# Up-projection of a gated MLP: seven block products for all three float32r parts instead of the mixed parts only

## The chip, the cores and the metric

The kernel runs on one core of one Trainium2 chip. The metric is the device time of one execution in microseconds (us); less is better. A run of the kernel before took 2623.07 us in the median.

## The reference

A decoder of two layers, 1,024 tokens, model width 1,024, all in float32: differential attention, then a gated MLP; forgetting attention, then a gated MLP. The change is in the MLP, which runs twice:

```python
def conv_ffn(x, w_in, conv_w, conv_b, w_out):
    u = x @ w_in                       # 1024 x 1024 times 1024 x 5632
    u = causal depthwise convolution of width 3 over the tokens, + conv_b
    gate, val = jnp.split(u, 2, axis=-1)
    return (jax.nn.gelu(gate) * val) @ w_out      # 2816 = 22 * 128
```

x is normalised (RMS norm with a gain) before it, and the output after it.

## The kernel before, in words

**Number format.** TensorE multiplies float32r, a float32 of reduced precision. To keep float32 accuracy every operand is split into two float32r parts, high = round(x) and low = x - high. A product is then three matmuls: high*high, high*low, low*high. One matmul has a 128x128 weight tile, 512 tokens, and sums into one bank of PSUM (128 x 512 float32); there are eight banks.

**Tiles.** `ffn` (L466) goes over 22 pairs j (`NJ`), each of one block of 128 gate columns (v = 0) and one of 128 value columns (v = 1). The 1,024 inputs are eight blocks `kc` of 128 rows; the tokens are two halves of 512. A pair fills four banks, c11, c12 (gate, first and second half), c21, c22 (value); even pairs use banks 0 to 3, odd pairs 4 to 7. So a pair can start while the results of the one before are read.

**Plain pairs** (0 and 1, `products`, L512): 4 quarters x 8 blocks x 3 parts = 96 matmuls.

**Pairs 2 to 21** (`winograd`, L521): the pair is taken as a 2x2 block product, rows gate/value, inner dimension split into blocks 0 to 3 and 4 to 7, columns the token halves. The Strassen-Winograd scheme forms it from seven products of blocks instead of eight. The kernel uses it for the two mixed parts only: `low` (L533) issues one of the seven products for high*low and low*high, 8 matmuls. The high*high part is added in the ordinary way by `main` (L540), four times 8 matmuls. GpSimd forms four weight sums per pair out of the split parts, for the high and the low parts separately (`sums`, L483, 8 instructions of 128x512, one pair ahead); the token sums (`token_sums`, L497) are formed once per layer, 32 instructions. VectorE combines the products in PSUM (`add`, L548).

**After a pair**, `act` (L572) applies the convolution: one ScalarE instruction (L576) and two VectorE `scalar_tensor_tensor` (STT, L578) per half of the pair, gelu on ScalarE (L582), the product gate*value on VectorE (L586), and a store to DRAM.

**Weights.** `Weights` (L30) loads raw float32 tiles of 512 KB from the SyncE queue (`wr`, two buffers) and splits each: high on ScalarE (L73), low on VectorE (L75). The parts have eight buffers `w`: two pairs.

**Tokens.** In front of the MLP `early` (L355) and `second_half` transpose the normalised stream on TensorE (L216), the first half of the tokens during the output projection, the second half after the first halves of the plain pairs. For each block ScalarE writes the high part out of PSUM (L231) and VectorE the low part, with PSUM as one input (L232). These 16 tiles, and e, f, y, the weight sums and more, come out of one pool of 28 buffers, `t`.

**Order.** A planner places the instructions on their engines at build time: it takes the earliest written instruction that is ready by its own costs, and each engine then runs its list strictly in order. Waits are semaphores. The pool buffers limit how far the list of one engine runs ahead.

**Down-projection** (`sweeps`, L374) follows, with all eight banks: for each of four blocks of tokens two banks in turn, the first block with banks 0 and 1.

Of the kernel before, what the change touches and what calls it, by code (L numbers as in the profile page):

```python
# [14 lines left out]
P = 128  # L15
# [8 lines left out]
EPS = 1e-6  # L24
SUB_EPS = 1e-5
LAM0 = 0.8 - 0.6 * math.exp(0.0)
NBUF = {"x": 16, "wr": 2, "w": 8, "t": 28}


class Weights:  # L30
# [6 lines left out]

    def load(self, n):
        while self.loaded < min(n, len(self.reqs)):
            ap, gain, shape = self.reqs[self.loaded]  # L40
            size = shape[0] * shape[1]
            t = self.k.tile("wr", tag="wr")
            self.k.loading = self.k.nc.sync.dma_start(out=t[:, :size], in_=ap)
            self.raw[self.loaded] = t
            self.loaded += 1
            self.gained(self.loaded - 1)

    def gained(self, n):

        while self.gains < n:  # L50
            _, gain, shape = self.reqs[self.gains]
# [38 lines left out]
class Kernel:  # L90
# [119 lines left out]
    def transposes(self, xs, half, kcs, banks, gain):  # L210

        nc = self.nc
        for i, kc in enumerate(kcs):
            b = banks[i % len(banks)]
            for t in range(4):
                nc.tensor.transpose(  # L216
                    self.ps[:, b * HALF + t * P:b * HALF + (t + 1) * P], xs[t][:, kc * P:(kc + 1) * P], self.ident
                )
            if half == 0:
                if kc == 0:  # L220
                    self.xh, self.xl = [], []
                self.xh.append(self.tile("xh", F32R, tag=self.x_tag))
                self.xl.append(self.tile("xl", F32R, tag=self.x_tag))
# [5 lines left out]
            else:  # L229
# [2 lines left out]
                nc.vector.scalar_tensor_tensor(  # L232
                    out=lo, in0=self.bank(b), scalar=g, in1=hi, op0=ALU.mult, op1=ALU.subtract
                )


    def load_post(self, gpost):
# [228 lines left out]
    def ffn(self, l, gpost, h_in, h_out, gain, final):  # L466


        nc = self.nc
        conv = self.const.tile([P, 2 * NJ, 4], F32, tag="conv", name=f"conv{l}")  # L470
        nc.sync.dma_start(out=conv, in_=self.a["conv"][l])
        g_dram = self.dram.tile([2, NJ, P, HALF], F32, name=f"g{l}")
        w_t, s_t = {}, {}
        t_c = {}
        toks = [slice(0, HALF), slice(HALF, S)]
# [7 lines left out]
        def sums(j):  # L483

            t = [self.tile("ws", F32R, [P, 2, 4, P]) for _ in range(4)]
            op = nc.gpsimd.tensor_tensor
            for i in range(2):
                g, v = w_t[j][0][i], w_t[j][1][i]
                a11, a12, a21, a22 = g[:, 0:4], g[:, 4:8], v[:, 0:4], v[:, 4:8]
                s1, s2, s3, s4 = (x[:, i] for x in t)  # L490
                op(out=s1, in0=a21, in1=a22, op=ALU.add)  # L491
                op(out=s2, in0=s1, in1=a11, op=ALU.subtract)  # L492
                op(out=s3, in0=a11, in1=a21, op=ALU.subtract)  # L493
                op(out=s4, in0=a12, in1=s2, op=ALU.subtract)
            s_t[j] = t

        def token_sums(eng, i, kcs):  # L497

            x = (self.xh, self.xl)[i]
            for kc in kcs:  # L500
                b11, b12 = (x[kc][:, c] for c in toks)
                b21, b22 = (x[kc + 4][:, c] for c in toks)
                t12, t34 = (self.tile("xs", F32R, [P, 2, HALF], tag="x") for _ in range(2))
                t_c[i, kc] = [t12[:, 0], t12[:, 1], t34[:, 0], t34[:, 1]]
                t1, t2, t3, t4 = t_c[i, kc]
                op = eng.tensor_tensor
                op(out=t1, in0=b12, in1=b11, op=ALU.subtract)
                op(out=t2, in0=b22, in1=t1, op=ALU.subtract)
                op(out=t3, in0=b22, in1=b12, op=ALU.subtract)
                op(out=t4, in0=b21, in1=t2, op=ALU.subtract)  # L510

        def products(j, v, half):  # L512
            wh, wl = w_t[j][v]
            b = 4 * (j % 2) + 2 * v + half
            for kc in range(8):
                for i, (w, x) in enumerate(((wh, self.xh), (wh, self.xl), (wl, self.xh))):
                    nc.tensor.matmul(  # L517
                        self.bank(b), w[:, kc], x[kc][:, toks[half]], start=kc == 0 and i == 0, stop=kc == 7 and i == 2
                    )

        def winograd(j):  # L521
            base = 4 * (j % 2)
            c11, c12, c21, c22 = (self.bank(base + i) for i in range(4))
            (gh, gl), (vh, vl) = w_t[j]
            s = s_t.pop(j)
            e = self.tile("e", shape=[P, 2, HALF])
            f = self.tile("f", shape=[P, 2, HALF])
            x = lambda half, k0: ([self.xh[k0 + k][:, toks[half]] for k in range(4)],
                                  [self.xl[k0 + k][:, toks[half]] for k in range(4)])
            sw = lambda n: (s[n - 1][:, 0], s[n - 1][:, 1])  # L530
            tw = lambda n: [[t_c[i, k][n - 1] for k in range(4)] for i in range(2)]

            def low(o, w, b, start=False):  # L533
                n = 0
                for k in range(4):
                    for i in range(2):
                        nc.tensor.matmul(o, w[i][:, k], b[1 - i][k], start=start and n == 0, stop=n == 7, skip_group_check=not start)  # L537
                        n += 1

            def main(o, w, half, start=False):  # L540
                for k in range(8):
                    nc.tensor.matmul(  # L542
                        o, w[:, k], self.xh[k][:, toks[half]], start=start and k == 0, stop=k == 7,
                        skip_group_check=not start,
                    )

            g = (gh, gl)
            add = lambda out, a, b: nc.vector.tensor_tensor(out=out, in0=a, in1=b, op=ALU.add)  # L548
            low(c11, [t[:, 0:4] for t in g], x(0, 0), True)
# [12 lines left out]
            main(c12, gh, 1)  # L562
            add(c12, c12, f[:, 0])
            act(j, 0)
            add(c21, c21, f[:, 1])
            main(c22, vh, 1)
            add(c22, c22, e[:, 1])
            act(j, 1)

        g_t = {}  # L570

        def act(j, v):  # L572
# [7 lines left out]
                )  # L580
            if v == 0:
                nc.scalar.activation(out=y, in_=y, func=AF.Gelu_apprx_tanh)  # L582
                g_t[j] = y
            else:
                g = g_t.pop(j)
# [21 lines left out]
            for v in (0, 1):  # L607
                products(j, v, 0)
        self.second_half((1, 3, 5, 7))
        token_sums(nc.gpsimd, 1, (2, 3))  # L610
        for j in range(NJ):
            if j > 0:
                weights(j + 1)
            if j < 2:
                if j == 1:
                    sums(2)
                    token_sums(nc.vector, 1, (0, 1))
                    token_sums(nc.vector, 0, range(4))
                for v in (0, 1):
                    products(j, v, 1)  # L620
                    act(j, v)
            else:
                if j + 1 < NJ:
                    sums(j + 1)
                else:
                    self.sweeps_begin(source, NJ, gpost, h_in, h_out, final)
                winograd(j)
            w_t.pop(j)
        self.sweeps(NJ, gain, final)


# [570 lines left out]
    def requests(self):  # L1202
# [34 lines left out]
        def ffn(l):  # L1237
            for j in range(NJ):
                for g in range(2):
                    r.append((a["ffn_in"][l, 2 * j + g], None, whole))  # L1240
# [152 lines left out]
```

## Time and profile before

| | |
|---|---|
| median of 3 runs | 2623.07 us (2622.27 to 3161.32) |
| the profiled execution | 2620.13 us, span 2618.3 us |
| PE busy | 2537.9 us, 97% of the span |
| DVE (VectorE), ACT (ScalarE), POOL (GpSimd) busy | 1673.3, 1073.0, 895.4 us |
| mean granted TensorE clock | 0.991 of full speed |
| first MLP up-projection, second one | from 568.63 us, from 1911.81 us |

How to read it: PE is TensorE's matmuls, PEld its weight loads. Busy shares are means over the span, so stretches are looked at one by one. Times of rows count from the start of the span. A row of the timeline gives the start, the time taken, engine, line, operation, output<-inputs, the count, and in square brackets the idle time of the engine before it with what released it. A matmul's own time (0.39 us) overlaps with the next one's; the distance between starts is the pace.

### The profile page before, as it was taken

The numbers are of one execution on the slowest core, as the hardware profiler recorded it, in microseconds if no ns is written. First come the engines' busy times: TensorE is split into PE (matmuls) and PEld (weight loads), VectorE is DVE, ScalarE is ACT, GpSimd is POOL, SyncE is SP. The second block draws the span as 40 slices with busy tenths as digits, with TensorE's granted clock in tenths as the row PEclk, the third lists the DMA queues.
The fourth block names the chain that finished last, engine by engine and source line by source line (L and its number), as shares of the span: only waits on it lengthen the run. The fifth ranks groups of instructions, "written<-read, shape, count | busy, mean of one in ns | idle before, by whom it ended". The sixth has DMA issues, their size and how long they took to land. (4 is left out here: it accounts for less than half of the span.)

```text
span 2618.3 us, 34308 instructions
## 1 busy us (share of the span) xinstructions
PE 2537.9 (97%) x13013; PEld 2152.3 (82%) x13013; DVE 1673.3 (64%) x2586; ACT 1073.0 (41%) x1857; POOL 895.4 (34%) x1050
## 2 busy tenths in 40 slices
PE   8999999998999999999999999998998999999998
PEld 7898998786888888888878888876887888888887
DVE  5767677558766767252567877776467676675253
ACT  4555555333323324242445555557332332234232
POOL 1222223227655661010322333223237666550000
PEclk9999999999999999999999999998999999999999
DMA  4111212341222225353312322225412222235353
GB/s 161 43 43 51 55 50 80 109 144 57 84 83 75 81 81 176 131 203 118 116 59 48 57 71 68 50 49 112 154 57 89 73 81 81 81 112 186 110 211 113
DMA packets 119866, 249.00 MB, mean 95 GB/s; under 512 B 34035, under 2 KB 50196, under 8 KB 119700
## 3 DMA queue, kind: packets, MB, share of 16 engines
q1 hardware_dynamic: 119700, 246.81, 29.5%
q8 instruction: 102, 1.67, 0.3%
q14 instruction: 64, 0.52, 0.1%
HBM read 197.85 MB, written 48.92 MB: 94 GB/s over the span
## 5 line engine op out<-in xcount | busy, mean ns | idle before, releaser
L73 ACT CAST wh<-wr 128x1024 fp32r<-128x1024 f32 (+1 forms) x240 | 252.3, 1052 | 800.3 <-PE ps L542 449.2
L75 DVE TENSOR_TENSOR wl<-wr,wh 128x1024 fp32r<-128x1024 f32 (+1 forms) x236 | 301.9, 1281 | 329.4 <-ACT wh L73 271.0
L267 PE MATMUL ps<-wh,src 128*128 128x512 f32 x1408 | 377.1, 389 | 0.0
L542 PE MATMUL ps<-xh,wh 128*128 128x512 f32 x1280 | 310.2, 389 | 1.9 <-DVE y L578 1.9
L267 PEld LDWEIGHTS ps<-wh,src 128*128 128x128 f32 x1408 | 264.2, 188 | 54.7
L542 PEld LDWEIGHTS ps<-xh,wh 128*128 128x128 f32 x1280 | 240.1, 188 | 52.4 <-issue 2.7
L537 PE MATMUL ps<-xs,ws 128*128 128x512 f32 x960 | 235.4, 394 | 16.6 <-POOL ws L492 16.6
L776 POOL CAST qz<-qs 64x128 fp32r<-64x128 f32 x256 | 84.4, 332 | 474.3 <-PE ps L765 439.3
L537 PEld LDWEIGHTS ps<-xs,ws 128*128 128x128 f32 x960 | 182.9, 191 | 55.8 <-POOL ws L492 17.5
L578 DVE SCALAR_TENSOR_TENSOR y<-ps,conv,y 128x1023 f32<-128x1023 f32 (+1 forms) x176 | 220.5, 1273 | 1.3
L267 PE MATMUL ps<-wl,src 128*128 128x512 f32 x704 | 216.7, 389 | 0.0
L204 POOL TENSOR_SCALAR post<-post 128x1 f32<-128x1 f32 x56 | 21.9, 392 | 560.0 <-ACT f L208 559.6
L650 PE MATMUL ps<-xh,wh 128*128 128x512 f32 x512 | 208.2, 407 | 4.8 <-DVE qs L671 4.4
L650 PE MATMUL ps<-xh,wl 128*128 128x512 f32 x512 | 201.4, 393 | 0.0
L650 PE MATMUL ps<-xl,wh 128*128 128x512 f32 x512 | 201.3, 393 | 0.0
L806 DVE TENSOR_TENSOR ptl<-ps,pth 128x512 fp32r<-128x512 f32 (+3 forms) x288 | 152.9, 552 | 60.3 <-ACT pth L805 58.1
L805 ACT CAST pth<-ps 128x512 fp32r<-128x512 f32 (+3 forms) x288 | 131.0, 478 | 63.0 <-PE ps L795 53.4
L267 PEld LDWEIGHTS ps<-wl,src 128*128 128x128 f32 x704 | 132.2, 188 | 27.4
L717 PE MATMUL ps<-wh,xh 128*128 128x256 f32 (+1 forms) x512 | 149.1, 292 | 1.4 <-DVE f L327 0.8
L717 PE MATMUL ps<-wh,xl 128*128 128x256 f32 (+1 forms) x512 | 146.4, 287 | 0.1
L491 POOL TENSOR_TENSOR ws<-wh 128x512 fp32r<-128x512 f32 x40 | 55.5, 1387 | 263.3 <-ACT wh L73 263.3
L717 PE MATMUL ps<-wl,xh 128*128 128x256 f32 (+1 forms) x512 | 145.4, 286 | 0.0
(200 smaller groups left out, 5788.8 us busy)
## 6 DMA issues: line engine op xcount, KB each, us to landing
wr<-in_ffn_in_dram SPq DMA_DIRECT2D x88, 512.0 KB, 3.5
wr<-in_ffn_out_dram SPq DMA_DIRECT2D x88, 512.0 KB, 3.9
g<-y SPq DMA_DIRECT2D x44, 512.0 KB, 2.8
g<-g SPq DMA_DIRECT2D x44, 512.0 KB, 7.0
h<-hold SPq DMA_DIRECT2D x24, 512.0 KB, 2.8
hold<-h SPq DMA_DIRECT2D x24, 512.0 KB, 6.8
crow<-c SPq DMA_DIRECT2D x16, 512.0 KB, 7.4
xraw<-in_x_dram SPq DMA_DIRECT2D x8, 512.0 KB, 6.6
```

Of the source, the lines that this page charges most:

```text
L73: self.k.nc.scalar.copy(out=hi[:, :size], in_=raw[:, :size])
L75: eng.tensor_tensor(out=lo[:, :size], in0=raw[:, :size], in1=hi[:, :size], op=ALU.subtract)
L267: nc.tensor.matmul(self.bank(2 * t + c), s[:, sp, t * P:(t + 1) * P], wt[:, 0, c * HALF:(c + 1) * HALF], start=first and wt is wh and sp = ...
L491: op(out=s1, in0=a21, in1=a22, op=ALU.add)
L537: nc.tensor.matmul(o, w[i][:, k], b[1 - i][k], start=start and n == 0, stop=n == 7, skip_group_check=not start)
L542: nc.tensor.matmul(o, w[:, k], self.xh[k][:, toks[half]], start=start and k == 0, stop=k == 7, skip_group_check=not start,)
L578: nc.vector.scalar_tensor_tensor(out=y[:, k:], in0=ps[:, :S - k], scalar=cw[:, 2 - k:3 - k], in1=y[:, k:], op0=ALU.mult, op1=ALU.add)
L650: nc.tensor.matmul(self.bank(b), w[:, kc], x[kc][:, c], start=kc == 0 and i == 0, stop=kc == 7 and i == 2)
L717: nc.tensor.matmul(o, x[kc][:, tb * P:(tb + 1) * P], w[:, kc % 4], start=kc == 0 and i == 0, stop=kc == 7 and i == 2,)
L776: op.tensor_copy(out=tile[up], in_=made["QS"][c][up, i * P:(i + 1) * P])
L805: nc.scalar.copy(out=hi, in_=src)
L806: nc.vector.tensor_tensor(out=lo, in0=src, in1=hi, op=ALU.subtract)
```

## The change

- All three parts go through the seven products: `part` issues 4 blocks x 3 parts = 12 matmuls, seven times per pair; `low` and `main` go.
- Weight sums are formed on the raw float32 tiles and split afterwards: 4 GpSimd sums of 128x512 per pair, then 4 casts on ScalarE and the low parts, three on VectorE (1,024, 512 and 1,024 columns) and one on GpSimd (1,024). The raw weight tiles of these pairs are used as they are and not split by `Weights`; the value's first half isn't split at all.
- Token blocks are kept raw too (`quarter`): one instruction copies the block out of PSUM with its gain (ScalarE for even blocks, VectorE for odd ones), ScalarE writes the high part, VectorE the low part, both from SBUF. Token sums are formed once on the raw blocks (16 instructions, half on GpSimd, half on VectorE) and split (8 casts, 8 subtractions, half of them on GpSimd).
- Three plain pairs instead of two. `sums` of the first seven-product pair is issued at the beginning of the third.
- The value half of a pair is convolved first, then the gate half. One combining addition less.
- The convolution's constants have one buffer for both layers.

```diff
+PLAIN = 3
@@ Weights.make
+            if len(self.reqs[i]) > 3:
+                self.done[i] = raw[:, :size].rearrange("p (a b) -> p a b", a=shape[0])
+                self.split += 1
+                continue
@@ transposes
+            if self.x_tag == "t":
+                self.quarter(self.bank(b), half, kc, self.gain[:, gain, kc:kc + 1])
+                continue
+    def quarter(self, ps, half, kc, g):
...
+        raw = self.xw[half, k][:, kc // 4]
+        t = self.xq[kc, half] = self.tile("xq", F32R, [P, 2, HALF])
+        if kc % 2 == 0:
+            nc.scalar.activation(out=raw, in_=ps, func=AF.Copy, scale=g)
+        else:
+            nc.vector.tensor_scalar(out=raw, in0=ps, scalar1=g, scalar2=None, op0=ALU.mult)
+        self.turned = nc.scalar.copy(out=t[:, 0], in_=raw)
+        nc.vector.tensor_tensor(out=t[:, 1], in0=raw, in1=t[:, 0], op=ALU.subtract)
@@ ffn
+        def split(raw, tag, eng=None):
+            hi, lo = (self.tile(n, F32R, [P, raw.shape[1], P], tag=tag) for n in ("sh", "sl"))
+            nc.scalar.copy(out=hi, in_=raw)
+            (eng or nc.vector).tensor_tensor(out=lo, in0=raw, in1=hi, op=ALU.subtract)
+            return hi, lo
+        def sums(g, v):
...
+            op(out=s1, in0=a21, in1=a22, op=ALU.add)
+            op(out=s2, in0=s1, in1=a11, op=ALU.subtract)
+            op(out=s3, in0=a11, in1=a21, op=ALU.subtract)
+            op(out=s4, in0=a12, in1=s2, op=ALU.subtract)
+            gp = split(g, "w")
+            vt = self.tile("vt", F32R, [P, 2, 4, P], tag="w")
+            nc.scalar.copy(out=vt[:, 0], in_=a22)
+            nc.vector.tensor_tensor(out=vt[:, 1], in0=a22, in1=vt[:, 0], op=ALU.subtract)
+            p12, p34 = split(s12, "t"), split(s34, "t", nc.gpsimd)
...
+        def token_sums(k):
...
+            op = (nc.gpsimd if k % 2 == 0 else nc.vector).tensor_tensor
...
+            for n, t, eng in ((1, t12, nc.vector), (3, t34, nc.gpsimd)):
+                hi, lo = (self.tile(x, F32R, [P, 2, HALF], tag="x") for x in ("th", "tl"))
+                nc.scalar.copy(out=hi, in_=t)
+                eng.tensor_tensor(out=lo, in0=t, in1=hi, op=ALU.subtract)
@@ winograd
+            def part(o, w, x, start):
+                for k in range(4):
+                    for i, (wi, xi) in enumerate(((0, 0), (0, 1), (1, 0))):
+                        nc.tensor.matmul(
+                            o, w[wi][:, k], x[k][xi], start=start and k == 0 and i == 0, stop=k == 3 and i == 2,
...
+            part(c11, a["a11"], b(0, 0), True)
             nc.scalar.copy(out=e[:, 0], in_=c11)
-            main(c21, vh, 0, True)
-            low(c11, [t[:, 4:8] for t in g], x(0, 4))
-            main(c11, gh, 0)
-            low(c22, sw(2), tw(2), True)
+            part(c22, a[2], t(2), True)
             add(f[:, 0], c22, e[:, 0])
-            low(c12, sw(1), tw(1), True)
-            add(e[:, 1], c12, e[:, 0])
-            low(c21, [t[:, 4:8] for t in (vh, vl)], tw(4))
-            low(c22, sw(3), tw(3))
+            part(c11, a["a12"], b(0, 4), False)
+            part(c22, a[3], t(3), False)
             add(f[:, 1], c22, e[:, 0])
-            low(c12, sw(4), x(1, 4))
-            main(c12, gh, 1)
+            part(c12, a[1], t(1), True)
+            add(c22, c12, f[:, 1])
+            part(c21, a["a22"], t(4), True)
+            add(c21, c21, f[:, 1])
+            part(c12, a[4], b(1, 4), False)
             add(c12, c12, f[:, 0])
+            act(j, 1)
             act(j, 0)
-            add(c21, c21, f[:, 1])
-            main(c22, vh, 1)
-            add(c22, c22, e[:, 1])
-            act(j, 1)
@@ ffn, the loop over the pairs
             if j < 2:
-                if j == 1:
-                    sums(2)
-                    token_sums(nc.vector, 1, (0, 1))
-                    token_sums(nc.vector, 0, range(4))
+                for k in (2 * j, 2 * j + 1):
+                    token_sums(k)
...
+            if j < PLAIN:
                 for v in (0, 1):
+                    if j >= 2:
+                        products(j, v, 0)
                     products(j, v, 1)
                     act(j, v)
```

## Rows read from the trace of the kernel before

**Rows 1.** The page: busy us, share of the span, instructions of each engine.

```profile
PE 2537.9 (97%) x13013; PEld 2152.3 (82%) x13013; DVE 1673.3 (64%) x2586; ACT 1073.0 (41%) x1857; POOL 895.4 (34%) x1050
```

**Rows 2.** Stretches: us, busy us (count) of each engine, granted clock, DMA share, GB/s.

```profile
620.00:640.00 20.00, 11.50 (x39) 8.97 (x40) 18.73 (x21) 3.53 (x4) 19.92 (x9) 0.74 0.28 103
800.00:900.00 100.00, 100.00 (x443) 82.84 (x442) 68.25 (x66) 29.80 (x30) 60.84 (x41) 1.00 0.23 80
```

**Rows 3.** Waits of PE, 540 to 700 us: total us, times, longest.

```profile
PE ps L537 <- POOL ws L492: 8.3, 1, 8.3
```

**Rows 4.** Timeline of PE in the two up-projections: start, us, engine, line, count.

```profile
568.63 0.48 PE L517 MATMUL ps<-xh,wh 128*128 128x512 f32 x1
...
595.35 0.50 PE L517 MATMUL ps<-xh,wh 128*128 128x512 f32 x1
...
620.19 2.09 PE L542 MATMUL ps<-xh,wh 128*128 128x512 f32 x8 [0.97 <-DVE y L578]
...
630.82 6.06 PE L537 MATMUL ps<-xs,ws 128*128 128x512 f32 x15 [8.31 <-POOL ws L492]
...
809.01 0.39 PE L537 MATMUL ps<-xl,wh 128*128 128x512 f32 x1
...
828.96 0.39 PE L537 MATMUL ps<-xl,wh 128*128 128x512 f32 x1
...
1028.42 0.62 PE L267 MATMUL ps<-wh,src 128*128 128x512 f32 x2
...
1911.81 0.48 PE L517 MATMUL ps<-xh,wh 128*128 128x512 f32 x1
...
2370.75 0.61 PE L267 MATMUL ps<-wh,src 128*128 128x512 f32 x2
```

**Rows 5.** Groups by shape: busy us, mean ns of one, idle before.

```profile
L494 POOL TENSOR_TENSOR ws<-wh,ws 128x512 fp32r<-128x512 f32 x40 | 51.8, 1295 | 0.0
L75 POOL TENSOR_TENSOR wl<-wr,wh 128x1024 fp32r<-128x1024 f32 x4 | 10.3, 2567 | 10.8 <-ACT wh L73 10.8
...
L75 DVE TENSOR_TENSOR wl<-wr,wh 128x1024 fp32r<-128x1024 f32 x234 | 299.4, 1280 | 321.0 <-ACT wh L73 262.6 <-PE ps L537 47.8 <-issue 6.6
L507 DVE TENSOR_TENSOR xs<-xh 128x512 fp32r<-128x512 f32 x8 | 5.4, 680 | 0.0
...
L73 ACT CAST wh<-wr 128x1024 fp32r<-128x1024 f32 x238 | 250.1, 1052 | 791.5 <-PE ps L542 449.2 <-PE ps L267 242.9 <-issue 28.4
L252 ACT CAST src<-g 128x512 fp32r<-128x512 f32 x88 | 49.4, 617 | 27.6 <-DMA g<-g 27.6
L550 ACT COPY e<-ps 128x512 f32<-128x512 f32 x40 | 23.0, 576 | 0.0
```

**Rows 6.** Timeline of DVE at a pair's end, and at the layer's end.

```profile
827.34 0.70 DVE L548 TENSOR_TENSOR ps<-ps,f 128x512 f32<-128x512 f32 x1 [2.20 <-PE ps L542]
...
832.14 3.78 DVE L578 SCALAR_TENSOR_TENSOR y<-ps,conv,y 128x1022 f32<-128x1022 f32 x3
836.02 2.20 DVE L586 TENSOR_TENSOR y<-y,y 128x1024 f32<-128x1024 f32 x1
838.22 0.69 DVE L548 TENSOR_TENSOR f<-ps,e 128x512 f32<-128x512 f32 x1
...
1034.54 1.28 DVE L578 SCALAR_TENSOR_TENSOR y<-ps,conv,y 128x1022 f32<-128x1022 f32 x1
```

**Rows 7.** Timeline of DVE and POOL at the entry of the up-projection.

```profile
572.61 1.40 DVE L232 SCALAR_TENSOR_TENSOR xl<-ps,gain,xh 128x512 fp32r<-128x512 f32 x2
...
600.22 1.78 DVE L508 TENSOR_TENSOR xs<-xl,xs 128x512 fp32r<-128x512 f32 x1
...
599.71 1.74 POOL L510 TENSOR_TENSOR xs<-xl,xs 128x512 fp32r<-128x512 f32 x1
...
619.95 8.37 POOL L493 TENSOR_TENSOR ws<-wh,wh 128x512 fp32r<-128x512 f32 x1
```

**Rows 8.** DMA issues: KB each, median us from issue to landing.

```profile
wr<-in_ffn_in_dram SPq DMA_DIRECT2D x88, 512.0 KB, 3.5
```

More of the change, by code (lines that the diff above doesn't have):

```diff
@@ L39, in load @@
         while self.loaded < min(n, len(self.reqs)):
-            ap, gain, shape = self.reqs[self.loaded]
+            ap, gain, shape = self.reqs[self.loaded][:3]
             size = shape[0] * shape[1]
@@ L50, in gained @@
         while self.gains < n:
-            _, gain, shape = self.reqs[self.gains]
+            gain, shape = self.reqs[self.gains][1:3]
             if gain is not None:
@@ L234, in transposes @@
                 )
+    def quarter(self, ps, half, kc, g):
+        nc = self.nc
+        if half == 0 and kc == 0:
+            self.xq, self.xw = {}, {}
+        k = kc % 4
+        if (half, k) not in self.xw:
+            self.xw[half, k] = self.tile("xw", shape=[P, 2, HALF], tag="tx"[half])
+        raw = self.xw[half, k][:, kc // 4]
[6 more added lines that the diff above has]
+        nc.vector.tensor_tensor(out=t[:, 1], in0=raw, in1=t[:, 0], op=ALU.subtract)
     def load_post(self, gpost):
@@ L497, in token_sums @@
[L497 to L510, printed above, removed]
+                if j >= PLAIN:
+                    w_t[j] = sums(*w_t[j])
@@ new lines, in split @@
+        def split(raw, tag, eng=None):
[4 more added lines that the diff above has]
+        def sums(g, v):
+            a11, a12, a21, a22 = g[:, 0:4], g[:, 4:8], v[:, 0:4], v[:, 4:8]
+            s12, s34 = (self.tile("ws", shape=[P, 8, P]) for _ in range(2))
+            s1, s2, s3, s4 = s12[:, 0:4], s12[:, 4:8], s34[:, 0:4], s34[:, 4:8]
+            op = nc.gpsimd.tensor_tensor
+            op(out=s1, in0=a21, in1=a22, op=ALU.add)
[7 more added lines that the diff above has]
+            p12, p34 = split(s12, "t"), split(s34, "t", nc.gpsimd)
+            lower = lambda p: [t[:, 0:4] for t in p]
+            upper = lambda p: [t[:, 4:8] for t in p]
+            return {
+                "a11": lower(gp), "a12": upper(gp), "a22": [vt[:, 0], vt[:, 1]],
+                1: lower(p12), 2: upper(p12), 3: lower(p34), 4: upper(p34),
+            }
@@ L515, in products @@
             for kc in range(8):
-                for i, (w, x) in enumerate(((wh, self.xh), (wh, self.xl), (wl, self.xh))):
+                x = self.xq[kc, half]
+                for i, (w, n) in enumerate(((wh, 0), (wh, 1), (wl, 0))):
                     nc.tensor.matmul(
-                        self.bank(b), w[:, kc], x[kc][:, toks[half]], start=kc == 0 and i == 0, stop=kc == 7 and i == 2
+                        self.bank(b), w[:, kc], x[:, n], start=kc == 0 and i == 0, stop=kc == 7 and i == 2
                     )
@@ L523, in winograd @@
             c11, c12, c21, c22 = (self.bank(base + i) for i in range(4))
-            (gh, gl), (vh, vl) = w_t[j]
-            s = s_t.pop(j)
+            a = w_t[j]
             e = self.tile("e", shape=[P, 2, HALF])
             f = self.tile("f", shape=[P, 2, HALF])
-            x = lambda half, k0: ([self.xh[k0 + k][:, toks[half]] for k in range(4)],
-                                  [self.xl[k0 + k][:, toks[half]] for k in range(4)])
-            sw = lambda n: (s[n - 1][:, 0], s[n - 1][:, 1])
@@ L531, in winograd @@
-            tw = lambda n: [[t_c[i, k][n - 1] for k in range(4)] for i in range(2)]
-            def low(o, w, b, start=False):
-                n = 0
-                for k in range(4):
[L536 to L545, printed above, removed]
@@ L547, in winograd @@
-            g = (gh, gl)
-            add = lambda out, a, b: nc.vector.tensor_tensor(out=out, in0=a, in1=b, op=ALU.add)
-            low(c11, [t[:, 0:4] for t in g], x(0, 0), True)
+            b = lambda half, k0: [(self.xq[k0 + k, half][:, 0], self.xq[k0 + k, half][:, 1]) for k in range(4)]
+            t = lambda n: [t_c[n, k] for k in range(4)]
+            def part(o, w, x, start):
+                for k in range(4):
+                    for i, (wi, xi) in enumerate(((0, 0), (0, 1), (1, 0))):
+                        nc.tensor.matmul(
+                            o, w[wi][:, k], x[k][xi], start=start and k == 0 and i == 0, stop=k == 3 and i == 2,
+                            skip_group_check=not start,
+                        )
@@ L582, in act @@
                 nc.scalar.activation(out=y, in_=y, func=AF.Gelu_apprx_tanh)
+            if j not in g_t:
                 g_t[j] = y
@@ L609, in ffn @@
         self.second_half((1, 3, 5, 7))
-        token_sums(nc.gpsimd, 1, (2, 3))
         for j in range(NJ):
```

43 lines of the change are left out of this document (24 added, 19 removed).

## Prediction

> **What bounds the kernel now.** I read the busy shares first: TensorE (PE) has work for 97% of the span [rows 1]. Such a share is a mean, so next come the stretches. Inside the up-projection PE is busy 100% of 100 us at the full granted clock, with VectorE (DVE) at 68, ScalarE (ACT) at 30 and GpSimd (POOL) at 61 us; only the 20 us where the seven-product pairs begin look different, 11.5 us busy and a mean clock of 0.74 [rows 2]. The waits name the cause: the first such pair waited 8.3 us for POOL's weight sums [rows 3]. The timeline gives the pace. From one pair to the next are 828.96 - 809.01 = 19.95 us [rows 4] for 88 matmuls (seven quarter products of 8 for the low parts, four of 8 for hh), 0.2267 us each. So up to the stall and after it the time is a count of matmuls.
>
> How much the stall costs: layer 0 takes 1028.42 - 568.63 = 459.79 us from its first up-projection matmul to its first down-projection matmul [rows 4]. Its 2 x 96 + 20 x 88 = 1,952 matmuls need 442.5 us; the transposes after the first 96 take 595.35 - 568.63 - 96 x 0.2267 = 4.96. That leaves 12.3 us: 8.31 + 0.97 idle and 3.0 at a lower clock, since the 15 matmuls after the stall took 6.06 us where 15 x 0.2267 is 3.4 [rows 4]. In layer 1 the same count gives 458.94 - 447.5 = 11.5 us. Together 23.8 us.
>
> **The change, part by part.** *Matmuls.* A pair with seven products for all three parts has 7 x 4 x 3 = 84 matmuls, four fewer than 88; 19 pairs per layer have it. The third plain pair has 96 instead of 88. Per layer 3 x 96 + 19 x 84 = 1,884, that is 68 fewer; for both layers 136 x 0.2267 = 30.8 us less. All of it lies on the path, because PE is the engine that is full [rows 2].
>
> *The stall at the first seven-product pair.* With three plain pairs that pair starts 192 matmuls after the second half's transposes, 595.35 + 43.5 = 638.9 us, where it now starts at 617 and finds its sums ready at 630.8 [rows 4]. POOL's work ahead of it becomes 8 token sums at 1.30 us [rows 5], four subtractions of 128x1024 at 2.57 [rows 5], then four weight sums and one more such subtraction: 10.4 + 10.3 + 7.8 = 28.5 us. DVE's instructions with two SBUF inputs in that time are eight quarter subtractions and eight token sums at 0.68, six subtractions of 1,024 columns at 1.28 and two products at up to 2.20 [rows 5, 6]: 10.9 + 7.7 + 4.4 = 23 us. Where both run such work at once they take 1.78 and 1.74 us a piece [rows 7], so I add them: 51.5 us, times 1.76/(0.68 + 1.30) = 0.89, 46 us from about 597, so 643. The last subtraction is needed 36 matmuls into the pair, at 647. I take the 23.8 us as won and set 1 us per layer against it; the ends are 0 and all 12.
>
> The trace lets the two engines slow each other (0.68 to 1.78 us), and once POOL stood 8.37 us in one sum [rows 7]. The Trainium skill's "GPSIMD Engine Reference", Key points, says that GpSimd shares its SBUF interfaces with VectorE and contends with VectorE instructions that have two SBUF inputs; the trace agrees. It speaks against the change, which turns a subtraction with a PSUM input into one with two SBUF inputs: by it the entry (next part) would cost its upper ends, 5.4 us more in all than I take.
>
> *The entry: raw quarter, then its high and low part.* Three instructions per block of tokens replace two. In the first half the four last blocks matter: DVE's last low part ends at 572.61 + 1.40 = 574.0, just when PE comes to it (568.63 + 22 x 0.2267 = 573.6) [rows 4, 7]. DVE gets two more copies of 0.70 and ACT two copies and four casts of 0.62 [rows 5]: bounds 0 and 2.6 us, and I take 1.5, since two DVE instructions stand in line there. In the second half DVE does 8 x 0.68 + 4 x 0.70 = 8.2 us in place of 5.6: bounds 0 and 2.6, and I take 1, as PE uses one block in 0.68 us and DVE makes one in 1.03 with a start of some 3 us. With the 1 us above, 3.5 us per layer, 7 in all.
>
> *The steady pair.* DVE: two low parts of 1,024 and one of 512 columns (3.2 us) replace two of 1,024 (2.6), one addition of 0.70 goes; per 19.04 us its load stays near 13.6. ACT gets 1.7 us more (3.7 of casts for 2.1), 7.6 in all; POOL falls from 12 to 7.8. All hide behind PE's 19.04. SP's two loads per pair, 3.5 us to landing [rows 8], now wait until POOL has read the raw tiles: 3.5 + 4 x 1.30 + 2.6 = 11.3 us per turn, under 19.04 as well. What can show is one deadline. The addition f0 = c22 + e is ready after 24 matmuls (5.44 us) and PE wants c22 again after 36 (8.16). Now it is ready after 40 and wanted after 56, and DVE reaches it at 838.22, right behind the product of the pair before [rows 6]. In the new order DVE has behind the pair's end one addition (done at 0.9), three STT of 1.26 (4.7), one split of 1.28 (6.0), then f0 (6.7): 1.5 us early. Bounds 0 and 2.7 us per pair (below); I take 0.1, times 38 pairs 4 us. The copy e on ACT, 0.58 us long [rows 5], has 2.72 us where it had 1.8.
>
> *Into the down-projection.* The gate half now comes last, and its banks are wanted 24 matmuls after the hand-over (5.4 us); DVE's last STT ends now 1034.54 + 1.28 - 1028.42 = 7.4 us after it [rows 4, 6], and two of the four move some 2.5 us ahead. Bounds 0 and 2, taken 0.5 per layer.
>
> **Sum.** 2620.1 (profiled execution; span 2618.3) - 30.8 - 23.8 + 7 + 4 + 1 = 2577.5. The median of the runs shown stands 2.9 us above the profiled execution, so 2580.
>
> **Rivals.** *Nothing new costs time*: 2620.1 - 30.8 - 23.8 + 2.9 = 2568, the least this change can reach. For it: ACT and POOL have room. Against it: DVE is already just in time at the entry [rows 7]. 15%.
>
> *The stall stays, moved to the fourth pair*: POOL's chain runs to 655 instead of 643 because DVE goes first, as in the 8.37 us row [rows 7]. The 23.8 us are not won: 2602. 12%. The Trainium skill's contention rule, named above, points this way; its size is in the rows only.
>
> *Slower: f0 late in every pair.* Place: DVE's queue behind the pair's end. If all three splits (3.2 us) and the product (2.20) [rows 5, 6] stand in front of f0, it ends at 4.7 + 3.2 + 2.2 + 0.7 = 10.8, 2.7 us after PE wants it; with the splits done earlier there is no loss. At 2 us and 38 pairs, 76 us: 2580 - 4 + 76 = 2652. It decides from (2623 - 2576)/38 = 1.24 us per pair on. For it: the order DVE now has puts the product in front of f0 [rows 6]. Against: 5.4 us idle-or-split time per pair is spread over 19 us, and splits may run one pair ahead. 13%; over 2675, 5%.
>
> *The change does not do what it says*: matmuls fall as counted but the new alternation of weights paces slower. In the rows every order of operands has the same 0.39 us, so 5%, with half the gain, 2595.
>
> **Forecast 55%.** Within it 2570 to 2592. The range that takes in the first two and most of the rest: 2566 to 2620, leaving out the slower case and a little more. Two per cent, about what a measurement of this kernel tells from no change, are 2570.6 and 2675.5: faster 0.15 (the first rival), slower 0.05, within 0.80.
>
> **What would show it.** Up-projection from its first matmul to the first of the down-projection: 459.8 down to about 436 us (1,884 x 0.2267 + 5 + 4). Pairs of 19.04 us with PE 100% busy show the steady step right; idle PE in front of the second c22 group, released by DVE, shows the slower rival; idle in front of the c22 group of the fourth pair, released by POOL or ACT, the second. A clock under 1 in the first 80 us of either FFN would mean that a stall is still there. The forecast is wrong if PE's pace is not 0.2267 us.

## The result, and the profile after

The changed kernel took 2581.6 us in the median of 4 runs (2579.96 to 2582.5); the kernel before took 2622.3 beside it. The ratio is 0.9846, 95% interval 0.9826 to 0.9865: 41 us less, clear of no change and inside 2%. Three executions that were far slower than all others (3161.32 and 6500.16 us of the kernel before, and 3176.98 us, the profiled one, of the run with fewer matmuls) are left out of every time here; the first of them is in the median of 2623.07 that the prediction started from. The forecast was 2580. Its sum was made of a gain and a price, and both have to be looked at, since the price was 15.6 us instead of 12 and lay elsewhere than I put it.

The profiled execution took 2582.5 us, with a span of 2580.7, 37.6 less than before. Its busy shares, in answer to [rows 1]:

```profile
PE 2509.5 (97%) x12877; PEld 2127.4 (82%) x12877; DVE 1714.1 (66%) x2566; ACT 1153.3 (45%) x1963; POOL 797.7 (31%) x928
```

PE has 136 matmuls and 28.4 us less to do, and the same share. The stretches of [rows 2], with the 20 us in which the seven-product pairs now begin (columns: us, then busy time of PE, PEld, DVE, ACT, POOL with their instructions, granted clock, DMA share, GB/s):

```profile
620.00:640.00 20.00, 20.00 (x90) 16.58 (x89) 18.94 (x15) 10.70 (x11) 15.74 (x7) 1.00 0.25 90
640.00:660.00 20.00, 17.08 (x63) 13.53 (x63) 14.52 (x12) 6.77 (x9) 16.74 (x10) 0.83 0.34 124
800.00:900.00 100.00, 100.00 (x443) 82.81 (x442) 78.60 (x70) 41.62 (x45) 52.53 (x26) 1.00 0.22 79
```

The steady stretch is full at the full clock. One dent is left, at 640 to 660: 2.9 us idle and a mean clock of 0.83, where before there were 8.5 us and 0.74. What PE waited for in the first up-projection (columns: what waited and for whom; us in total, times, longest; the rows left out belong to the attention and its projection in front of it):

```profile
PE ps L581 <- ACT e L588: 2.9, 1, 2.9
...
PE ps L565 <- DVE xq L260: 0.7, 1, 0.7
PE ps L222 <- DVE xw L258: 0.7, 1, 0.7
PE ps L565 <- ACT xw L256: 0.6, 1, 0.6
```

The wait for POOL of [rows 3] is gone. There are two things in its place: 2.0 us at the entry, three short waits for a block's raw copy or low part, and 2.9 us for e, the copy that ScalarE takes of c11 in the fourth pair. PE's timeline, in answer to [rows 4]:

```profile
567.96 0.71 PE L565 MATMUL ps<-xq,wh 128*128 128x512 f32 x2
...
640.51 0.62 PE L581 MATMUL ps<-xq,sh 128*128 128x512 f32 x2
...
649.04 1.22 PE L581 MATMUL ps<-xq,sh 128*128 128x512 f32 x2 [2.92 <-ACT e L588]
...
823.58 0.62 PE L581 MATMUL ps<-xq,sh 128*128 128x512 f32 x2
...
842.62 0.62 PE L581 MATMUL ps<-xq,sh 128*128 128x512 f32 x2
...
1008.44 0.62 PE L293 MATMUL ps<-wh,src 128*128 128x512 f32 x2
```

A pair takes 842.62 - 823.58 = 19.04 us, 84 x 0.2267. From the first matmul of the up-projection to the first of the down-projection are 1008.44 - 567.96 = 440.48 us, 19.3 less than before; in layer 1 439.33 (458.94 before). Together that is 38.9 less: the whole change lies in this stretch. By count it needs 1,884 x 0.2267 + 4.96 = 432.1 us, so 8.4 us are left over in layer 0 and 7.2 in layer 1, together the 15.6. In layer 0 the entry has 2.3 of them: 640.51 - 567.96 = 72.55 us up to the fourth pair, by count 288 x 0.2267 + 4.96 = 70.25. The fourth pair has the other 6.1: the 2.9 idle for e, and 2.9 at a lower clock behind it, since the 15 matmuls from 649.04 to 655.38 took 6.34 us where 15 x 0.2267 is 3.40. In layer 1 PE waited for the same four things as long, and the 15 matmuls behind e lost 1.8.

Why e was late is seen in ScalarE's timeline, and in VectorE's and GpSimd's behind it. The first product into c11 had its last matmul issued at 643.0, and PE wanted the bank again at 646.1 (649.04 - 2.92):

```profile
640.48 0.62 ACT L531 CAST vt<-wr 128x512 fp32r<-128x512 f32 x1 [0.42 <-DMA wr<-in_ffn_in_dram]
644.46 1.06 ACT L615 ACTIVATE y<-y 128x1024 f32<-128x1024 f32 x1 [3.36 <-DVE y L611]
645.43 1.19 ACT L609 ACTIVATE y<-ps,conv 128x1024 f32<-128x1024 f32 x1
646.52 1.98 ACT L515 CAST sh<-ws 128x1024 fp32r<-128x1024 f32 x2
648.40 0.58 ACT L588 COPY e<-ps 128x512 f32<-128x512 f32 x1
```

ScalarE was not busy: it stood idle for 3.36 us in front of the third pair's gelu, which waited for VectorE's convolution, and e was four instructions further down its list: behind the convolution of the value half and two casts, 3.0 us. The chain goes back further:

```profile
634.38 2.30 POOL L528 TENSOR_TENSOR ws<-wr,ws 128x512 f32<-128x512 f32 x1
...
636.71 1.06 ACT L515 CAST sh<-ws 128x1024 fp32r<-128x1024 f32 x1 [1.50 <-POOL ws L528]
...
639.00 2.39 DVE L516 TENSOR_TENSOR sl<-wr,sh 128x1024 fp32r<-128x1024 f32 x1 [0.96 <-ACT sh L515]
...
643.10 1.27 DVE L611 SCALAR_TENSOR_TENSOR y<-ps,conv,y 128x1022 f32<-128x1022 f32 x1
```

VectorE came to that convolution late, behind a subtraction that waited for a cast on ScalarE, and ScalarE's list had stood 1.50 us for GpSimd's last weight sum of the fourth pair. For PE itself GpSimd's sums, which the prediction feared here, were done in time:

```profile
628.10 3.35 POOL L555 TENSOR_TENSOR tl<-tw,th 128x1024 fp32r<-128x1024 f32 x1 [2.32 <-ACT th L554]
...
637.84 2.46 POOL L516 TENSOR_TENSOR sl<-ws,sh 128x1024 fp32r<-128x1024 f32 x1 [1.17 <-ACT sh L515]
```

The last subtraction ended at 640.3, where I had worked out 643, and it was needed 36 matmuls into the pair, at 640.5 + 8.2 = 648.7.

The deadline of the steady pair, f0, in VectorE's timeline, in answer to [rows 6]:

```profile
822.87 1.28 DVE L611 SCALAR_TENSOR_TENSOR y<-ps,conv,y 128x1022 f32<-128x1022 f32 x1
824.06 0.68 DVE L586 TENSOR_TENSOR f<-ps,e 128x512 f32<-128x512 f32 x1
824.65 1.65 DVE L516 TENSOR_TENSOR sl<-wr,sh 128x1024 fp32r<-128x1024 f32 x1
826.23 2.31 DVE L620 TENSOR_TENSOR y<-y,y 128x1024 f32<-128x1024 f32 x1
```

It ends at 824.74 and is wanted at 826.29, where the second product into c22 begins: 1.5 us early. The product of the pair before (L620) stands behind it here, in front of it in the kernel before.

### The profile page after: what moved, and what is told of

It is laid out like the page before. It is cut to its first block, busy times and chain, and to the rows that moved or that the text cites. A ratio compares the mean times of both kernels' runs of the same rounds, so it can differ in the third digit from the quotient of the medians.

```text
span 2580.7 us, 33993 instructions
## 1 busy us (share of the span) xinstructions
PE 2509.5 (97%) x12877; PEld 2127.4 (82%) x12877; DVE 1714.1 (66%) x2566; ACT 1153.3 (45%) x1963; POOL 797.7 (31%) x928
## 5 line engine op out<-in xcount | busy, mean ns | idle before, releaser
L81 DVE TENSOR_TENSOR wl<-wr,wh 128x1024 fp32r<-128x1024 f32 x160 | 205.7, 1286 | 275.4 <-ACT wh L79 268.8
L79 ACT CAST wh<-wr 128x1024 fp32r<-128x1024 f32 x164 | 172.2, 1052 | 335.4 <-PE ps L293 239.1
L581 PE MATMUL ps<-xq,sh 128*128 128x512 f32 x912 | 283.9, 393 | 5.8 <-ACT e L588 5.8
L609 ACT ACTIVATE y<-ps,conv 128x1024 f32<-128x1024 f32 x88 | 106.2, 1207 | 367.4 <-DVE ps L586 367.4
L688 PE MATMUL ps<-xh,wh 128*128 128x512 f32 x512 | 208.1, 407 | 5.8 <-DVE qs L709 4.9
L581 PEld LDWEIGHTS ps<-xq,sh 128*128 128x128 f32 x912 | 172.4, 189 | 43.0 <-ACT e L588 7.2
L581 PE MATMUL ps<-xq,sl 128*128 128x512 f32 x456 | 178.9, 392 | 0.0
L581 PE MATMUL ps<-th,sh 128*128 128x512 f32 x456 | 177.9, 390 | 0.0
L581 PE MATMUL ps<-tl,sh 128*128 128x512 f32 x456 | 177.7, 390 | 0.0
L581 PE MATMUL ps<-th,sl 128*128 128x512 f32 x456 | 177.4, 389 | 0.0
L843 ACT CAST pth<-ps 128x512 fp32r<-128x512 f32 (+3 forms) x288 | 131.2, 478 | 62.2 <-PE ps L833 54.6
```

Source lines behind the costliest of these rows:

```text
L81: eng.tensor_tensor(out=lo[:, :size], in0=raw[:, :size], in1=hi[:, :size], op=ALU.subtract)
L581: nc.tensor.matmul(o, w[wi][:, k], x[k][xi], start=start and k == 0 and i == 0, stop=k == 3 and i == 2, skip_group_check=not start,)
L609: nc.scalar.activation(out=y, in_=ps, func=AF.Identity, scale=cw[:, 2:3], bias=cw[:, 3:4])
L688: nc.tensor.matmul(self.bank(b), w[:, kc], x[kc][:, c], start=kc == 0 and i == 0, stop=kc == 7 and i == 2)
L843: nc.scalar.copy(out=hi, in_=src)
```

## The experiments

Times beside each other come from the same chip and share the runs of the kernel before (2620.3 in the first set, 2619.8 in the second, 2620.2 in the third). "Up-projection" is the stretch from its first matmul to the first of the down-projection, layer 0 and layer 1.

### Two plain pairs: is the third what removes the stall?

```diff
-PLAIN = 3
+PLAIN = 2
```

> The changed kernel with two plain pairs instead of three. Theory (time is the count of matmuls at 0.2267 us plus the waits of PE at the first seven-product pair): 16 matmuls fewer are 3.6 us less, but that pair now starts at about 617 us, while GpSimd ends its second weight sum at about 633 and the low part of it is there at 635.5; PE stands some 14 us per layer and loses 3 more to a lower clock, and the 10.9 us that both layers lose now to the late copy e go: 2581.6 - 3.6 - 10.9 + 34 = about 2601 us. Rival (the third plain pair wins nothing, since with it gone the sums are asked for and made earlier): 2578 us, waits of PE as now.

2598.8 us, ratio 0.9922 (0.9904 to 0.9940); up-projection 448.80 and 448.39. The size is that of the theory, which counted 16 matmuls fewer where it is 2 x 12 = 24, 5.4 us, and so should have said 2599. The releaser is not. What PE waited for:

```profile
PE ps L581 <- ACT th L554: 6.2, 1, 6.2
PE ps L581 <- DVE tl L555: 5.9, 2, 3.4
...
```

These are the splits of the token sums, on ScalarE and VectorE; the cast that PE waited 6.2 us for had itself stood 2.92 us for a token sum on GpSimd. Before, the token sums could be had from parts that existed; now they need a sum, a cast and a subtraction one after the other. So it is the whole preparation that wants the third plain pair's time, not GpSimd's weight sums alone.

### Four plain pairs: does a later start take the rest away?

```diff
-PLAIN = 3
+PLAIN = 4
```

> The changed kernel with four plain pairs. Theory: 24 matmuls more are 5.4 us more; the copy e of the first seven-product pair no longer stands behind late casts, because the entry's work on ScalarE and VectorE is done by then, so the 10.9 us of both layers (2.9 us idle each, the rest at the lower clock) go: 2576 us. Rival (the wait for e belongs to the first seven-product pair wherever it stands): 2587 us, with the same 2.9 us wait one pair later.

2575.96 us, ratio 0.9832 (0.9817 to 0.9848); up-projection 437.23 and 437.26. The wait for e is gone, PE is 100% busy at the full clock where the seven-product pairs begin, and only the entry's 2.0 us are left. In these two traces the fourth plain pair costs 12 matmuls more (2.7 us per layer) and saves more than that. The count is 1,896 x 0.2267 + 4.96 = 434.8, so the entry alone is worth 2.4 us per layer.

### The kernel before with three plain pairs

```diff
-            if j < 2:
+            if j < 3:
                 if j == 1:
-                    sums(2)
                     token_sums(nc.vector, 1, (0, 1))
                     token_sums(nc.vector, 0, range(4))
+                if j == 2:
+                    sums(3)
                 for v in (0, 1):
+                    if j == 2:
+                        products(j, v, 0)
                     products(j, v, 1)
```

> The kernel before with three plain pairs, its seven products for the mixed parts alone as they were. Theory (the third plain pair alone takes away the wait for GpSimd's sums, whatever they are made of): 16 matmuls more are 3.6 us more, the 23.8 us of stall and lower clock go: 2622.7 + 3.6 - 23.8 = 2602 us. Rival (the sums of split parts are too many for GpSimd beside VectorE, so the wait only moves to the fourth pair): 2626 us.

2603.2 us, ratio 0.9937 (0.9921 to 0.9953); up-projection 449.94 and 451.01, of which the count takes 1,960 x 0.2267 + 4.96 = 449.3. So 17 of the 41 us are had with the third plain pair alone, without a seven-product high part. The rest of the change goes from 2603.2 to 2581.6, 22 us. By count it should be worth 2 x 76 x 0.2267 = 34.5: this is the part that paid the new costs.

### Fewer matmuls, nothing else

In every seven-product pair three matmuls of the third part (low weights times high tokens) of one product are left out, 114 in all, so the output is not the reference's.

```diff
-            def part(o, w, x, start):
+            def part(o, w, x, start, third=True):
...
+                        if i == 2 and k < 3 and not third:
+                            continue
...
-            part(c21, a["a22"], t(4), True)
+            part(c21, a["a22"], t(4), True, False)
```

> The changed kernel with three of the four low*high matmuls of the product for c21 left out in every seven-product pair (that part of the sum is missing). Theory (PE alone sets the pair): 3 x 38 = 114 matmuls fewer at 0.2267 us are 25.8 us less, 2556 us. Rival (VectorE or ScalarE is so near its deadlines that a pair shorter by 0.68 us waits for f0 or e): half of it or less, 2569 us or more, with waits of PE in every pair.

2555.1 us in the mean of three runs (2553.0 to 2558.4), ratio 0.9752 (0.9735 to 0.9769): 26.3 less than the mean of the changed kernel's runs, and 24.6 by the two ratios, against 114 x 0.2267 = 25.8. As far as the runs resolve it, a matmul in a seven-product pair is worth its full 0.2267 us, and the rival's half is out. No trace of it is used, so that no pair waits is read from the time alone.

### The slower rival made to come true: the third split of a pair on VectorE

```diff
-            p12, p34 = split(s12, "t"), split(s34, "t", nc.gpsimd)
+            p12, p34 = split(s12, "t"), split(s34, "t")
```

> The changed kernel with the low part of the weight sums 3 and 4 on VectorE instead of GpSimd. VectorE's list then has that subtraction, the next pair's low part and the product gate*value in front of f0. Theory (the slower rival of the forecast, f0 late on VectorE): f0 now ends about 6.6 us into a pair and is wanted at 8.2; with 1.2 us more and the product of 1.2 to 2.3 in front it ends at about 9.8 to 11, so PE waits some 2.5 us in each of 38 pairs, 95 us: about 2676 us, every wait of PE put down to VectorE's f. Rival (there is room for one more subtraction, 16 of 19 us busy): 2582 us.

2604.7 us, ratio 0.9942 (0.9927 to 0.9956); up-projection 452.97 and 452.72. Slower than the changed kernel by some 23 us, and far from 2676. The waits in layer 0:

```profile
PE ps L581 <- DVE f L586: 8.8, 16, 0.8
...
```

VectorE's timeline in one pair:

```profile
829.09 1.41 DVE L516 TENSOR_TENSOR sl<-ws,sh 128x1024 fp32r<-128x1024 f32 x1
830.42 1.21 DVE L516 TENSOR_TENSOR sl<-wr,sh 128x1024 fp32r<-128x1024 f32 x1
831.55 2.31 DVE L620 TENSOR_TENSOR y<-y,y 128x1024 f32<-128x1024 f32 x1
833.78 0.68 DVE L586 TENSOR_TENSOR f<-ps,e 128x512 f32<-128x512 f32 x1
```

The mechanism is the rival's to the letter: splits and the product stand in front of f0, which ends at 834.46. The pair's first matmul into c11 starts at 822.95, so f0 comes 11.5 us into the pair, where the rival said 10.8 and PE would have wanted it at 8.2. PE's timeline shows why that cost so little:

```profile
822.95 0.62 PE L581 MATMUL ps<-xq,sh 128*128 128x512 f32 x2
...
825.67 0.39 PE L581 MATMUL ps<-th,sh 128*128 128x512 f32 x1
...
831.11 0.62 PE L581 MATMUL ps<-xq,sh 128*128 128x512 f32 x2
...
834.52 0.50 PE L581 MATMUL ps<-th,sh 128*128 128x512 f32 x1 [0.53 <-DVE f L586]
```

Between 825.67 and 831.11 there are 24 matmuls with token sums (th, tl), two products; in the changed kernel there are 13 from 820.63 to 823.58, one product and one matmul of another. The planner, which orders by its own costs, has put a whole further product, into c12, ahead of the one that needs f0. So f0 is wanted 11.0 us into the pair and PE waits 0.53. A pair takes 834.52 - 814.66 = 19.86 us, 0.82 longer (PE waited for the same thing at 814.66, a pair earlier). 16 of the 19 pairs have such a wait.

### Gate half convolved first, as before

```diff
-            act(j, 1)
             act(j, 0)
+            act(j, 1)
```

> The changed kernel with the gate half convolved before the value half, as in the kernel before. Theory: the gate half needs the last product of the pair, so all four STT start after the pair's end, and f0 stands behind them, one split and the product: it ends some 10 to 12 us into the pair in place of 6.6, PE waits 2 to 3.5 us in each of 38 pairs: 2660 to 2715 us. Rival (VectorE has time enough, the order of the halves is of no matter): 2582 us.

2612.3 us, ratio 0.9974 (0.9963 to 0.9985), about 31 us slower than the changed kernel, and clearly below the expected 2660. The waits from 568 to 1030 us:

```profile
PE ps L581 <- DVE f L586: 6.1, 7, 1.0
PE ps L293 <- ACT src L278: 3.1, 2, 1.9
PE ps L581 <- ACT e L588: 2.9, 1, 2.9
PE ps L581 <- DVE y L611: 1.9, 5, 0.4
...
```

Those for f0, for the convolution (y) and for the first source of the down-projection (src) are new, 11.1 us. The end of the up-projection has to be read with care, since the planner drew matmuls of the down-projection forward into the last pair:

```profile
1012.30 0.73 PE L293 MATMUL ps<-wh,src 128*128 128x512 f32 x2 [1.95 <-ACT src L278]
...
1024.96 0.39 PE L581 MATMUL ps<-xq,sl 128*128 128x512 f32 x1
```

The last up-projection matmul starts at 1024.96, against 1008.22 in the changed kernel; 13 matmuls of the down-projection (3 us) lie in front of it. So the stretch is some 13 us longer per layer, which the new waits nearly cover. The order of the halves, which the prediction used for its f0 deadline, is worth about 31 us of this change; of the theory's mechanism, f0 late in every pair, the trace shows 7 late pairs of 19 and two further waits that it did not have, and its price was more than twice too high.

### The parts of a token block straight from PSUM

```diff
-        if kc % 2 == 0:
-            nc.scalar.activation(out=raw, in_=ps, func=AF.Copy, scale=g)
-        else:
-            nc.vector.tensor_scalar(out=raw, in0=ps, scalar1=g, scalar2=None, op0=ALU.mult)
-        self.turned = nc.scalar.copy(out=t[:, 0], in_=raw)
-        nc.vector.tensor_tensor(out=t[:, 1], in0=raw, in1=t[:, 0], op=ALU.subtract)
+        self.turned = nc.scalar.activation(out=t[:, 0], in_=ps, func=AF.Copy, scale=g)
+        nc.vector.scalar_tensor_tensor(
+            out=t[:, 1], in0=ps, scalar=g, in1=t[:, 0], op0=ALU.mult, op1=ALU.subtract
+        )
+        nc.scalar.activation(out=raw, in_=ps, func=AF.Copy, scale=g)
```

> The changed kernel with the high and the low part of a token block made straight from PSUM, as before the change, and the raw copy written beside them on ScalarE. Theory (the chain of three instructions at the entry costs the 2 us idle per layer that PE shows there): about 4 us less, 2578 us, and the late e as it is. Rival (ScalarE's second copy holds the banks longer, so the transposes wait instead): 2582 us or more.

2577.3 us, ratio 0.9838 (0.9821 to 0.9854): the expected time, not clear of the changed kernel's 0.9846 (0.9826 to 0.9865), and what the traces show is another reason. The waits in layer 0 (the rows left out belong to the attention and its projection):

```profile
PE ps L222 <- ACT xw L259: 2.2, 3, 1.2
PE ps L580 <- ACT e L587: 2.0, 1, 2.0
...
PE ps L580 <- DVE f L585: 1.0, 1, 1.0
...
PE ps L564 <- ACT xw L259: 0.5, 1, 0.5
```

The entry got worse, 2.7 us for 2.0: the raw copy is now the last reader of the transposed block's bank, and the next transposes (L222) wait for it. The wait in the fourth pair did not get shorter either, it is split: 2.0 for e and 1.0 for f0, where it was 2.9. Up-projection 438.29 and 438.45, 2.2 and 0.9 less. What got better is the clock behind the wait, 1.00 in place of 0.83 (in layer 1, 1960 to 1980 us, 1.00 in place of 0.91):

```profile
640.00:660.00 20.00, 16.98 (x74) 13.40 (x73) 14.24 (x12) 6.71 (x8) 15.75 (x9) 1.00 0.38 133
```

Why it did not fall here stays open.

### e ahead on ScalarE

In the fourth pair, the third pair's value half (its convolution and what follows) and the casts of the next weight sums are placed after e on their engines' lists.

```diff
-            nc.scalar.copy(out=e[:, 0], in_=c11)
+            last = nc.scalar.copy(out=e[:, 0], in_=c11)
+            if j == PLAIN:
+                with self.tc.issue_after(last.ins):
+                    act(j - 1, 1)
+                weights(j + 1, last)
...
-            p12, p34 = split(s12, "t"), split(s34, "t", nc.gpsimd)
...
+                with self.tc.issue_after(last.ins):
+                    p12, p34 = split(s12, "t"), split(s34, "t", nc.gpsimd)
```

> The changed kernel with an order on ScalarE in the first seven-product pair of each layer: the copy e goes in front of the convolution of the third pair's value half and of the casts of the next pair's weight sums. Theory (e stands 2.9 us late behind these and the clock falls after it): the wait and the lower clock go, 10.9 us in both layers, about 2571 us. Rival (the next wait is right behind it, f0 or the products of the next pair, since these are now later): 2578 us or more.

2574.9 us, ratio 0.9830 (0.9816 to 0.9845); up-projection 436.40 and 436.43, 7 us less for both layers. The wait for e is gone, and the clock in 640 to 660 is back:

```profile
640.00:660.00 20.00, 18.61 (x81) 14.83 (x80) 16.31 (x13) 9.49 (x11) 17.10 (x9) 1.00 0.38 135
```

ScalarE's list around e:

```profile
647.34 1.06 ACT L623 ACTIVATE y<-y 128x1024 f32<-128x1024 f32 x1 [3.56 <-DVE y L619]
648.30 0.56 ACT L592 COPY e<-ps 128x512 f32<-128x512 f32 x1
```

The gelu still stands in front of e and still waits for VectorE, 3.56 us. Only the value half's convolution and the two casts are gone from there, and with them PE's wait. So with the same instructions on every engine, those 3.0 us in front of e in ScalarE's list were the wait of 2.9 and the lower clock behind it. A smaller wait came in its place, which the expectation did not have: 1.4 us for f0 on VectorE.

### Both edits, and both with the raw copies shared as before

The first kernel has the two edits above together. The second has the edit on e, and the raw copy behind the parts made by ScalarE for even blocks and by VectorE for odd ones.

> Both edits that gained by themselves: e placed ahead on ScalarE at the first seven-product pair, and the parts of each token block taken from PSUM with the raw copy on ScalarE. Theory, gains come from separate waits: the 1.4 us for f0 goes, because VectorE is rid of eight copies, the entry's idle rises from 2.0 to 2.7 us per layer as in the run with that edit alone, up-projection 436.4 - 1.4 + 0.7 = 435.7 us, time 2573.5 us. Rival, the two edits take away the same wait: the f0 wait stays, 437 us, 2576 us or more.

> As the run before, but the raw copy behind the two parts is made by ScalarE for even blocks and by VectorE for odd ones, so that each engine has the same instructions as in the changed kernel and only their order within a block differs. Theory, the entry is late because the raw copy stands ahead of the parts and because one engine alone has three instructions of a block: the entry's idle falls from 2.0 to about 1 us per layer, the f0 wait stays at 1.4, up-projection 435.4 us, 2573 us. Rival, the number of instructions per engine sets it: idle 2.0 us as before, 436.4 us, 2575 us.

2574.9 us (0.9826; 0.9813 to 0.9840) and 2576.1 us (0.9829; 0.9816 to 0.9843). In both, the wait for f0 is gone; the entry's idle time, all of it for raw copies on ScalarE, stands at 2.7 us in layer 0 and 1.7 in layer 1 in the first, and at 3.2 us in both layers in the second. Behind these short waits the clock fell: 0.93 in 600 to 620 us and 0.91 in 1900 to 1920 in the first, 0.91 in 580 to 600 and 0.83 in 1900 to 1920 in the second. The theories did not have that. Up-projection: 436.25 and 435.30; 436.21 and 437.49. For the first kernel the theory's 435.7 holds in the mean of the two layers, and the time does not tell it from the edit on e alone. For the second both theories fell, since neither had the entry above 2.0. Against the changed kernel these versions and the one with four plain pairs are 5 to 7 us shorter in the median, 0.2 to 0.3%; their intervals overlap with each other's and with the changed kernel's, so which is best stays open.

## Why the prediction was right, step by step

**Matmuls, -30.8: right.** Pace 19.04/84 = 0.2267 us, the page has 136 fewer, and the run with 114 fewer gave 24.6 to 26.3 for 25.8. The rival that the change does not do what it says is out.

**The stall, -23.8: right that it goes, by the third plain pair.** With two of them it comes back as 12 us of waits per layer, and the kernel before with three has none of it, only 0.2 and 1.3 us for e. The order of causes was incomplete: I looked at GpSimd's chain alone, and with two plain pairs PE waited for the token sums' splits on ScalarE and VectorE.

**Lateness of the fourth pair, 1 us per layer: the failed term.** It was 8.4 - 2.3 = 6.1 and 7.2 - 2.3 = 4.9. I priced GpSimd's sums, which had 8 us in hand, and wrote of e only that it had 2.72 us for 0.58 us of work. That is true in the steady pair. In the first seven-product pair e stands behind the last plain pair's convolution, gelu and the casts, in a list that runs strictly in order. The rival of a stall moved to the fourth pair named the right place and twice the size (11.5 and 12.3 us per layer). Its sign, idle time there released by GpSimd or ScalarE, came in front of the second product into c11 and not of c22, released by ScalarE. GpSimd was not what PE waited for, but its last weight sum is in the chain that made e late.

The contention it built on is real: the 128x1024 subtraction of GpSimd took 3.35 us above for 2.57 [rows 5], and over the steady stretch VectorE had 78.6 us per 100, 15.0 per pair, where I had counted 13.6; GpSimd had 10.0 for 7.8. In the steady pair all of it stayed behind PE's 19.04. At the border it did not: in the entry three low parts of 128x512 took 3.42 us beside token sums on GpSimd where one alone takes 0.68, and PE waited 0.7 us for one of them; and of the subtraction that stood in front of the late convolution, 2.39 us are shown above for 1.28 [rows 5].

```profile
598.32 3.42 DVE L260 TENSOR_TENSOR xq<-xw,xq 128x512 fp32r<-128x512 f32 x3
```

The Trainium skill's "GPSIMD Engine Reference", Key points, says that GpSimd shares its SBUF interfaces with VectorE and that instructions of VectorE with two SBUF inputs contend; the traces agree, with the 3.42 and 3.35 us above. How much of the 15.6 us is due to it no run shows.

**The entry, 2.5 us per layer: 2.3, of it 2.0 idle.** It was where I put it, in the blocks that PE reaches just as they are made. That VectorE's raw copies cause it was not shown: with all raw copies on ScalarE, behind the parts, the idle time rose.

**The steady pair, 4 us, and the hand-over, 1 us: both nothing.** The argument for f0 came out as worked (6.7 us into the pair forecast, 824.74 - 817.91 = 6.8 measured, where 817.91 is the pair's first matmul, three products in front of 826.29), and no pair waited. I had set 0.1 us per pair for a thing that has a margin of 1.5. In the hand-over no wait shows.

So 12 was the sum of 5 for the entry, 2 for the fourth pair, 4 and 1, and 15.6 that of 4.6 and 11.0: errors of -0.4, +9.0, -4 and -1 that partly cancel. The median also stands 0.9 us below the profiled execution, where I had added 2.9. That 2580 came within 2 us is luck; the gain of 54.6 us, from which the price goes off, was right as worked.

**The slower rival, 2652.** Its condition is one line of code away, and f0 then does come 11.5 us into the pair. Its price was wrong, 0.82 us in 16 of 19 pairs for 2 in each, because I took PE's order as given. With it the change would have been 2605 us, not slower than before.

**"Nothing new costs time", 2568.** The runs with e ahead come within 7 to 8 us of it. In the one with both edits, what is left of PE's waits is the entry, with the lower clock behind it.

## What to carry to other kernels

At the border between two kinds of loop body, read the list of every engine there, the idle ones too: a short instruction on an engine with 45% load delayed a full one, because it stood behind longer ones, and the first of them waited for a third engine. When a planner orders the instructions, price a late operand against the order that the planner would then choose, not against the one in the trace. Before a large change is credited, run its smallest part on the kernel before: here one more plain pair gave 17 of 41 us.

## What the runs showed of the hardware

A PE wait costs more than the idle time in its row. In the run with the third split on VectorE, 0.53 us idle made a pair 0.82 longer: the last matmul before it lasts 0.39 but would have been followed after 0.2267, which hides 0.16, and the first one after it took 0.33 to the next instead of 0.23.

The granted clock fell behind a short wait. After the 2.9 us for e, the matmuls of the changed kernel went on at the lower level, 1.2 GHz, and came back to 2.4 GHz while PE worked on without a pause:

```profile
652.62 0.63 PE L581 MATMUL ps<-xq,sl 128*128 128x512 f32 x1
653.04 1.05 PE L581 MATMUL ps<-xq,sh 128*128 128x512 f32 x2
...
655.38 0.40 PE L581 MATMUL ps<-th,sh 128*128 128x512 f32 x1
655.61 0.39 PE L581 MATMUL ps<-tl,sh 128*128 128x512 f32 x1
```

They stand 0.42 us apart for one matmul at 652.6 (granted clock 0.50 from 650 to 654 us) and 0.23 from 655.4 on. So the wait of 2.9 us lost 2.9 us more at the lower level. In layer 1 the same wait had a mean clock of 0.91 in its 20 us, 1.8 us more. In layer 0 of the run with the gate half first, the same wait of 2.9 us, with another of 1.0 soon behind it, lost nothing in this way:

```profile
640.00:660.00 20.00, 16.09 (x70) 12.66 (x69) 15.75 (x13) 7.16 (x9) 17.29 (x10) 1.00 0.38 130
```

What a wait loses at the lower clock is not fixed by its length, and a microsecond or two between two kernels can be that alone.
